# The down projection of a hybrid transformer block, transposed and with Strassen's scheme for every other pair of row tiles

## The chip, the cores and the metric

The kernel runs on one core of a Trainium2 chip. The core has five engines with a queue of instructions each: TensorE (PE) multiplies matrices, VectorE (DVE) and ScalarE (ACT) work on elements, GpSimd (POOL) does a little of the same, and SyncE (SP) issues most of the DMAs. The metric is the device time in microseconds. Three runs of the kernel before took 2153.89, 2154.22 and 2154.32 us; the median is 2154.22.

## The reference, cut to what matters

One block: RMSNorm, an input projection, a short convolution and a windowed attention side by side, an output projection with residual, then the MLP and a last norm. The change touches the MLP only:

```python
h = rms_norm(h_res, norm2_g[l])
h_res = h_res + jnp.square(jax.nn.relu(h @ w_up[l])) @ w_down[l]
out = rms_norm(h_res, final_norm_g)
```

There are 512 tokens, 2048 features and 8192 hidden features, all in fp32.

## The kernel before

Every fp32 operand is split in two parts that PE multiplies fast: a rounded one (hi, a CAST on ACT, line 182) and what is left (lo, a subtraction on DVE, line 183). A product takes three matmuls, hi x hi, hi x lo and lo x hi, which add up in one PSUM bank.

The up projection runs over 32 groups of 256 hidden features (`n`). A group takes four steps (`s`) over 512 input features each. A step loads one slab of weights, 512 KB (`load`, line 159, from SP), into one of three slots (`raw`), and uses one level of Strassen's scheme: DVE forms four sums of weight blocks (lines 747 to 749), ACT and DVE split the three blocks that are used as they are (`q`) and the four sums (`wsp`), and PE makes seven products of 128 x 128 weights with 256 tokens for each of two pairs of row tiles (lines 766 to 770). The operand on the token side stands ready in SBUF, eight pairs in eight places (`sobuf`, `xa`, `xc`). At the end of a group `up_out` combines four PSUM banks into the four quarters of the output (lines 778 to 786), applies relu and square on ACT (787, 788) and writes them to DRAM from ACT's queue (789, `a_d`, 512 KB). The banks alternate between two sets of four, `mm` and `aux`.

The down projection runs in eight chunks of eight row tiles, by four column blocks of 512 features. Its weights are the moving operand: a product takes 128 tokens of the activations as weights of the array and 512 features as columns (`mm3`, lines 633 to 635). The activations come back from `a_d` and are split once for each chunk. At the end of a chunk and column block DVE adds the banks to the residual `acc`, scaled by token (line 852). The last chunk also makes the sums of squares for the last norm and stores the output.

The order of the instructions on each engine is fixed before the run by the framework's list scheduler, which also hands out the slots of the rings: a slot goes to the tiles in the order in which they ask for it. On the chip each engine takes its instructions in that order. In the tables of instructions below `u12_3` is PSUM bank 3 of group 12, `raw_up13_0` the weights of group 13, step 0, as loaded, `q3` and `wsp` the split weights, `xq` and `ctmp` the buffers in which a group's output is combined.

Of the kernel before, what the change touches and what calls it, by code (L numbers as in the profile page):

```python
# [8 lines left out]
F32 = mybir.dt.float32  # L9
# [4 lines left out]
P = 128  # L14
D = 2048
# [84 lines left out]
def hybrid_block_kernel(  # L100
# [53 lines left out]
    wring = {}  # L154


    def load(src, name):
        raw = wring["raw"].next(name)
        wring["last"] = nc.sync.dma_start(raw, src)
        return raw  # L160

# [205 lines left out]


    xap = tc.alloc_tile_pool(name="xap", bufs=1, side="left")
    xa_hi = xap.tile([P, 8, SEQ], F32R, name="xa_hi")  # L370
    xa_lo = xap.tile([P, 8, SEQ], F32R, name="xa_lo")
    xe = tc.alloc_tile_pool(name="xe", bufs=1, side="left")
    xc2 = []

    def xc_tiles(pool, n):
        for i in range(n):
            f = len(xc2)
            hi = pool.tile([P, 2, SEQ], F32R, name=f"xc_hi{f}")
# [346 lines left out]
    a_d = [dram.tile([P, 4 * HT], F32, name=f"a_d{n}") for n in range(NG)]  # L725


    PROD = {
# [9 lines left out]

    by4 = lambda v, n=4: v.rearrange("p (m s c) -> p m s c", m=2, s=n)

    def up_slab(n, s):
        raw = load(w_up[n, s], f"up{n}_{s}")
# [7 lines left out]
        t_hi, t_lo = (by4(v) for v in part_tiles(f"up{n}_{s}"))  # L750
        split(t_hi, t_lo, t)
        return (q_hi, q_lo), (t_hi, t_lo)

    def up_step(bs, n, s):
        both = up_slab(n, s)
        for k in range(2):
            m = 2 * s + k
            for q, (sm, w, x, b, c) in PROD.items():
                o = bs[b][:, c * HT : (c + 1) * HT]
                h, l = (v[:, k, w, :] for v in both[sm])  # L760
                xh, xl = (operand[m][x][:, i, :] for i in range(2))
                first = m == 0 and q in (1, 2, 3, 5)
                if q == 5:

                    x2 = operand[m][x].rearrange("p h c -> p (h c)")
                    nc.tensor.matmul(bs[b], lhsT=h, rhs=x2, start=first, stop=False, skip_group_check=True)  # L766
                else:
                    nc.tensor.matmul(o, lhsT=h, rhs=xh, start=first, stop=False, skip_group_check=True)  # L768
                    nc.tensor.matmul(o, lhsT=h, rhs=xl, start=False, stop=False, skip_group_check=True)  # L769
                nc.tensor.matmul(o, lhsT=l, rhs=xh, start=False, stop=m == NPR - 1, skip_group_check=True)  # L770

    def up_out(bs, n):


        e, u = E.next()
        e, u = (v.rearrange("p (s c) -> p s c", c=HT) for v in (e, u))
        two = lambda v: v.rearrange("p (a b) -> p a b", a=2)
        nc.scalar.copy(u[:, 0, :], bs[2][:, :HT])
        nc.vector.tensor_tensor(u[:, 1, :], bs[0][:, :HT], u[:, 0, :], op=ALU.add)
        nc.vector.tensor_tensor(e[:, 0, :], bs[2][:, HT:], u[:, 1, :], op=ALU.add)  # L780
        nc.scalar.copy(e[:, 2, :], bs[3][:, HT:])
        nc.vector.tensor_tensor(e[:, 2, :], bs[3][:, :HT], e[:, 2, :], op=ALU.add)
        nc.vector.tensor_tensor(e[:, 1, :], e[:, 2, :], u[:, 1, :], op=ALU.subtract)
        nc.vector.tensor_tensor(e[:, 2, :], e[:, 2, :], e[:, 0, :], op=ALU.subtract)
        nc.vector.tensor_tensor(e[:, 3, :], bs[0][:, HT:], u[:, 0, :], op=ALU.add)
        nc.vector.tensor_tensor(e[:, 0:2, :], two(bs[1]), e[:, 0:2, :], op=ALU.add)
        nc.scalar.activation(e, e, AF.Relu)
        nc.scalar.activation(e, e, AF.Square)
        nc.scalar.dma_start(a_d[n], e.rearrange("p s c -> p (s c)"))
# [17 lines left out]
    xcp.release()  # L807
    xe.release()
    xap.release()
    wp2 = ctx.enter_context(tc.tile_pool(name="wp2", bufs=1, side="left"))  # L810
    wring["raw"] = Ring(*raw_slots(3, wp), *raw_slots(2, wp2))
    wring["split"] = Ring(*split_slots(3, wp), *split_slots(3, wp2))
    A = Ring(*[lambda name, i=i: part(sobuf, 2048, i) for i in range(7)])
    pf = ctx.enter_context(tc.tile_pool(name="pf", bufs=1, side="left"))
    gF = pf.tile([P, D], F32, name="gF")
    sq = pf.tile([P, NT, 5], F32, name="sq")
    junk = [pf.tile([P, 512], F32, name=f"junk{i}") for i in range(2)]

    QUART = {(1, 1): 0, (0, 0): 1, (1, 0): 2, (0, 1): 3}
    tags = ["mm", "aux"]  # L820
    turn = 0
    for ch in range(NCHUNK):
        a_hi, a_lo = [], []
        last = ch == NCHUNK - 1
        k0 = ch * FCH
        if last:
            with tc.issue_after(wring["last"].ins):
                nc.sync.dma_start(gF, final_g.partition_broadcast(P))
        for i in range(3 if last else 4):
            bs = [bank(tags[turn], f"d{ch}_{i}_{t}") for t in range(NT)]  # L830
            turn ^= 1
            for s_ in range(0, FCH, 2):
                if i == 0:

                    n = 4 * ch + s_ // 2
                    both = A.next()
                    split(both[:, 0:1024], both[:, 1024:2048], load(a_d[n], f"a{n}"))
                    for b in range(2):
                        for lst, c in ((a_hi, 0), (a_lo, 1024)):
                            lst.append([both[:, c + QUART[t // 2, b] * HT + t % 2 * P :][:, :P] for t in range(NT)])  # L840
                wh, wl = slab(w_down[i, (k0 + s_) // 2], 512, f"dn{ch}_{i}_{s_}")
                if ch == 0 and s_ == 2:

                    with tc.issue_after(wring["last"].ins):
                        nc.sync.dma_start(accs[i], acc_d[i])
                for k in range(2):
                    kt = s_ + k
                    for t in range(NT):
                        mm3(bs[t], a_hi[kt][t], a_lo[kt][t], wh[:, k, :], wl[:, k, :], kt == 0, kt == FCH - 1)
            for t in range(NT):  # L850
                a = acc(i, t)
                nc.vector.scalar_tensor_tensor(a, bs[t], rs2[:, t : t + 1], a, op0=ALU.mult, op1=ALU.add)  # L852

                if last:
# [7 lines left out]
    for t in range(NT):  # L862
# [89 lines left out]
```

## Time and profile before

| | |
|---|---|
| median of the runs | 2154.22 us |
| the profiled execution | 2152.87 us |
| its span, first to last instruction | 2151.1 us |
| PE busy | 2138.4 us (99%), 13404 matmuls |
| DVE busy | 1294.5 us (60%) |
| ACT busy | 810.3 us (38%) |
| POOL busy | 141.0 us (7%) |
| DMA | 261.29 MB, 121 GB/s |

Busy times are sums over the whole span, and the span has several stages. Matmuls are pipelined: a record of one lasts longer than the step from one start to the next, so the rate is counted from the number of matmuls in a stretch. The up projection lies about between 801 and 1445 us, the down projection between 1445 and 2142 us.

### The profile page before, as it was taken

How to read it: one execution, taken by the hardware profiler on the slowest of the kernel's cores; microseconds unless marked ns; L12 is line 12 of the kernel's file. 1: busy time of each engine (PE TensorE's matmuls, PEld its weight loads, DVE VectorE, ACT ScalarE, POOL GpSimd, SP SyncE). 2: the span in 40 equal slices, each digit the busy share in tenths (PEclk: the TensorE clock that was granted, in tenths of full speed). 3: DMA queues.
4: the chain of work that ended last, by engine and by line, in shares of the span. 5: the costliest groups of instructions: out<-in, count | busy, mean ns of one | idle time of the engine just before them, and what ended most of it. 6: DMA issues, size and time to landing. Idle time of an engine off the chain costs nothing.

```text
span 2151.1 us, 32786 instructions
## 1 busy us (share of the span) xinstructions
PE 2138.4 (99%) x13404; PEld 1940.3 (90%) x13404; DVE 1294.5 (60%) x2047; ACT 810.3 (38%) x1142; POOL 141.0 (7%) x256
## 2 busy tenths in 40 slices
PE   9999999999999999999999999999999999999998
PEld 8999999999988889999999999998888888888887
DVE  7776766443435569888888888874444343434434
ACT  6455544222212335545545545552222222222223
POOL 1432321001110000000000000000000000000001
PEclk9999999999999999999999999999999999999999
DMA  5322222222253334434334334355343333433422
GB/s 193 91 91 82 75 87 75 92 94 92 96 167 108 118 120 135 138 128 137 130 126 138 133 123 137 138 194 218 117 134 105 125 127 108 137 118 118 148 88 79
DMA packets 89996, 261.29 MB, mean 121 GB/s; under 512 B 25637, under 2 KB 25717, under 8 KB 88693
## 3 DMA queue, kind: packets, MB, share of 16 engines
q1 hardware_dynamic: 84660, 238.22, 33.6%
q10 hardware_dynamic: 4608, 16.78, 1.9%
q0 software_dynamic: 576, 4.19, 0.5%
q8 instruction: 105, 1.72, 0.3%
q14 instruction: 47, 0.38, 0.1%
HBM read 233.99 MB, written 25.17 MB: 120 GB/s over the span
## 4 chain that ended last, share of the span: by engine, by line
PE 98%; POOL 1%; SPq 0%; DMA 0%; ACT 0%; issue 0%; POOLq 0%; ACTq 0%; DVE 0%
PE d L633 10%; PE d L634 10%; PE d L635 10%; PE u L770 10%; PE u L768 9%; PE u L769 9%; PE u L766 3%; PE mm_u L211 1%; PE mm_c L211 1%; PE mm_u L208 1%; PE mm_c L208 1%; PE mm_u L209 1%; PE mm_c L209 1%; PE mm_b L211 1%; PE mm_b L208 1%; PE mm_b L209 1%
## 5 line engine op out<-in xcount | busy, mean ns | idle before, releaser
L633 PE MATMUL d<-wsp_dn,sobuf 128*128 128x512 f32 x992 | 385.9, 389 | 0.0
L634 PE MATMUL d<-wsp_dn,sobuf 128*128 128x512 f32 x992 | 385.9, 389 | 0.0
L635 PE MATMUL d<-wsp_dn,sobuf 128*128 128x512 f32 x992 | 385.9, 389 | 0.0
L183 DVE TENSOR_TENSOR wsp_dn<-raw_dn,wsp_dn 128x1024 fp32r<-128x1024 f32 x124 | 151.7, 1224 | 267.2 <-ACT wsp_dn L182 267.1
L182 ACT CAST wsp_dn<-raw_dn 128x1024 fp32r<-128x1024 f32 x124 | 130.6, 1054 | 379.4 <-PE d L635 375.0
L635 PEld LDWEIGHTS d<-wsp_dn,sobuf 128*128 128x128 f32 x992 | 186.2, 188 | 38.7
L633 PEld LDWEIGHTS d<-wsp_dn,sobuf 128*128 128x128 f32 x992 | 186.2, 188 | 38.7
L634 PEld LDWEIGHTS d<-wsp_dn,sobuf 128*128 128x128 f32 x992 | 186.2, 188 | 38.6
L182 ACT CAST q<-raw_up 128x768 fp32r<-128x768 f32 x128 | 106.8, 835 | 234.9 <-PE u L769 165.3
L183 DVE TENSOR_TENSOR wsp_up<-tsum,wsp_up 128x1024 fp32r<-128x1024 f32 x128 | 156.7, 1224 | 44.2 <-ACT wsp_up L182 43.9
L182 ACT CAST wsp_up<-tsum 128x1024 fp32r<-128x1024 f32 x128 | 134.3, 1049 | 69.7 <-PE u L770 60.9
L183 DVE TENSOR_TENSOR q<-raw_up,q 128x768 fp32r<-128x768 f32 x128 | 122.4, 956 | 41.6 <-ACT q L182 41.6
L770 PE MATMUL u<-sobuf,wsp_up 128*128 128x256 f32 x512 | 144.9, 283 | 0.0
L769 PE MATMUL u<-sobuf,q 128*128 128x256 f32 x384 | 108.9, 284 | 0.0
L768 PE MATMUL u<-sobuf,wsp_up 128*128 128x256 f32 x384 | 108.6, 283 | 0.0
L768 PE MATMUL u<-sobuf,q 128*128 128x256 f32 x384 | 108.4, 283 | 0.0
L769 PE MATMUL u<-sobuf,wsp_up 128*128 128x256 f32 x384 | 108.4, 282 | 0.0
L770 PE MATMUL u<-sobuf,q 128*128 128x256 f32 x384 | 108.3, 282 | 0.0
L852 DVE SCALAR_TENSOR_TENSOR acc<-d,few,acc 128x512 f32<-128x512 f32 x124 | 86.1, 748 | 24.0 <-PE d L635 24.0
L183 DVE TENSOR_TENSOR sobuf<-raw_a,sobuf 128x1024 fp32r<-128x1024 f32 x32 | 39.2, 1225 | 101.4 <-ACT sobuf L182 101.4
L770 PEld LDWEIGHTS u<-sobuf,wsp_up 128*128 128x128 f32 x512 | 97.1, 190 | 0.0
L747 DVE TENSOR_TENSOR tsum<-raw_up 128x512 f32<-128x512 f32 x128 | 88.1, 688 | 2.9 <-DMA raw_up<-in_w_up_dram 1.0
(319 smaller groups left out, 5469.9 us busy)
## 6 DMA issues: line engine op xcount, KB each, us to landing
raw_up<-in_w_up_dram SPq DMA_DIRECT2D x128, 512.0 KB
raw_dn<-in_w_down_dram SPq DMA_DIRECT2D x124, 512.0 KB
a_d<-xq ACTq DMA_DIRECT2D x32, 512.0 KB
raw_a<-a_d SPq DMA_DIRECT2D x32, 512.0 KB
raw_q<-in_w_in_dram SPq DMA_DIRECT2D x16, 512.0 KB
raw_u<-in_w_in_dram SPq DMA_DIRECT2D x16, 512.0 KB
raw_c<-in_w_in_dram SPq DMA_DIRECT2D x16, 512.0 KB
raw_b<-in_w_in_dram SPq DMA_DIRECT2D x16, 512.0 KB
```

The costliest lines, as they stand in the source:

```text
L182: first = nc.scalar.copy(hi, src)
L183: second = nc.vector.tensor_tensor(lo, src, hi.bitcast(F32), op=ALU.subtract)
L208: nc.tensor.matmul(b, lhsT=wh, rhs=cols(h_hi, kt), start=kt == 0, stop=False)
L209: nc.tensor.matmul(b, lhsT=wh, rhs=cols(h_lo, kt), start=False, stop=False)
L633: nc.tensor.matmul(o, lhsT=ah, rhs=wh, start=start, stop=False)
L634: nc.tensor.matmul(o, lhsT=ah, rhs=wl, start=False, stop=False)
L635: nc.tensor.matmul(o, lhsT=al, rhs=wh, start=False, stop=stop)
L747: nc.vector.tensor_tensor(t[:, :, 0:2, :], b12, w[:, :, 1:3, :], op=ALU.add)
L768: nc.tensor.matmul(o, lhsT=h, rhs=xh, start=first, stop=False, skip_group_check=True)
L769: nc.tensor.matmul(o, lhsT=h, rhs=xl, start=False, stop=False, skip_group_check=True)
L770: nc.tensor.matmul(o, lhsT=l, rhs=xh, start=False, stop=m == NPR - 1, skip_group_check=True)
L852: nc.vector.scalar_tensor_tensor(a, bs[t], rs2[:, t : t + 1], a, op0=ALU.mult, op1=ALU.add)
```

## The change

The first 24 of the 32 pairs of hidden row tiles (three quarters) leave the old chunks; chunks 6 and 7 stay as they were. For the 24 pairs the product is transposed: the weights are the array's weights and 256 or 512 tokens the columns, so that the result has features on the partitions.

- Eight column groups (`G`) of 256 features are visited in turn, 24 visits. Visit `v` takes group `v % 8` and the eight pairs `v` to `v + 7` (modulo 24), so that three visits of a group cover all pairs. From one visit to the next the set slides by one pair: `down_operand` loads and splits one new pair into the place of the old one.
- Even pairs go by Strassen's scheme: seven products of 256 columns with three matmuls each, with weight sums made by the function that made them for the up projection. Odd pairs go plainly, with products of 512 columns. A visit has two steps of each kind, with two pairs in a step: 84 matmuls of 256 columns and 48 of 512.
- `down_out` combines the four banks; the results add up in eight tiles `accT`. In chunk 6, 64 transposes (16 x 4) bring them back to tokens on partitions, and a second update for each bank adds them to `acc`.
- In the up projection, `up_out` keeps its operations, with the quarters in another order. After an even group below 24, POOL forms four combinations of the quarters, in a tile taken from the ring of the weight slots (`xs`), and writes them to DRAM from POOL's queue.
- In the last up group, the operands of the first eight pairs are loaded between its steps, also through the three weight slots.
- Buffers of the rest move: chunks 6 and 7 use parts of `xq` and `xa` as slots, and the last gain and scratch tiles lie where `xc` was.

```diff
+    NPD = 24
+    by_scheme = lambda n: n % 2 == 0
@@ up_out, after relu and square
+        nc.scalar.dma_start(a_d[n][:, :1024], e.rearrange("p s c -> p (s c)"))
+        if n < NPD and by_scheme(n):
+            raw = wring["raw"].next(f"xs{n}")
+            xs = by_q(raw)
+            nc.gpsimd.tensor_tensor(xs[:, 0, :], e[:, 0, :], e[:, 1, :], op=ALU.subtract)
+            nc.gpsimd.tensor_tensor(xs[:, 1, :], xs[:, 0, :], e[:, 2, :], op=ALU.subtract)
+            nc.gpsimd.tensor_tensor(xs[:, 2, :], e[:, 2, :], e[:, 0, :], op=ALU.subtract)
+            nc.gpsimd.tensor_tensor(xs[:, 3, :], e[:, 3, :], xs[:, 1, :], op=ALU.add)
+            nc.gpsimd.dma_start(a_d[n][:, 1024:], raw)
...
+    def down_operand(n):
+        if by_scheme(n):
+            v = places[n % NW // 2][0][2]
+            r = load(a_d[n][:, 256:1024], f"da{n}", 768)
+            split(v[:, 0:3, 0, :], v[:, 0:3, 1, :], by_q(r))
+            r = load(a_d[n][:, 1024:], f"ds{n}")
+            split(v[:, 3:7, 0, :], v[:, 3:7, 1, :], by_q(r))
+        else:
+            r = wring["raw"].next(f"da{n}")
...
+            both = whole[n % NW // 2]
+            split(both[:, 0:1024], both[:, 1024:2048], r)
...
+    def down_step(bs, pairs, G, begun, last, name):
+        raw = wring["raw"].next(name)
+        for k, n in enumerate(pairs):
+            wring["last"] = nc.sync.dma_start(
...
+        if by_scheme(pairs[0]):
+            both = step_slab(raw, name)
+            for k, n in enumerate(pairs):
+                ops = places[n % NW // 2][0][2]
+                for q, (sm, w, x, _, _) in PROD.items():
...
+                    mm(b, o, h, xh)
+                    mm(b, o, h, xl)
+                    mm(b, o, l, xh, last and k == 1)
+        else:
...
+                for e in range(2):
+                    xh, xl = (v[:, i * 1024 + e * 512 :][:, :512] for i in range(2))
+                    for j in range(2):
+                        b = 1 if j else 3
+                        mm(b, bs[b], hi[:, k, e, j, :], xh)
+                        mm(b, bs[b], hi[:, k, e, j, :], xl)
+                        mm(b, bs[b], lo[:, k, e, j, :], xh, last and k == 1 and e == 1)
...
         for s_ in range(4):
             up_step(bs, n, s_)
+            for m in {0: (0, 2), 1: (4, 6), 2: (1, 3, 5, 7)}.get(s_, ()) if n == NG - 1 else ():
+                down_operand(m)
         up_out(bs, n)
+    for v in range(NPD):
+        G = v % 8
+        bs = banks(v)
+        begun = set()
+        at = lambda *d: [(v + i) % NPD for i in d]
+        for s_, d in enumerate(((0, 2), (1, 3), (4, 6), (5, 7))):
+            down_step(bs, at(*d), G, begun, s_ > 1, f"dt{v}_{s_}")
+            if s_ == 0 and v + 1 < NPD:
+                down_operand((v + 8) % NPD)
...
+        if v < 8:
...
+            down_out(bs, accT[G], u)
+        else:
+            down_out(bs, e, u)
+            nc.vector.tensor_tensor(accT[G], accT[G], e, op=ALU.add)
...
+                if ch == first_ch:
+                    pt = bank(tags[turn], f"pt{i}_{t}")
+                    for k in range(4):
+                        v = accT[2 * i + k // 2][:, QUART_T[t // 2, k % 2], t % 2 * P : (t % 2 + 1) * P]
+                        nc.tensor.transpose(pt[:, k * P : (k + 1) * P], in_=v, identity=ident)
+                    nc.vector.scalar_tensor_tensor(a, pt, rs2[:, t : t + 1], a, op0=ALU.mult, op1=ALU.add)
```

The order on ACT where group 12 ends and group 13 begins. Before:

```order
L182 CAST q3_2_7852<-raw_up13_0_10699 128x768
L789 DMA a_d11_7866<-xq_6616 128x1024
L182 CAST wsp_up13_0_10706<-tsum_7850 128x1024
L182 CAST q3_3_7853<-raw_up13_1_10749 128x768
L182 CAST wsp_up13_1_10756<-tsum_7850 128x1024
L182 CAST q3_1_7851<-raw_up13_2_10799 128x768
L781 COPY xq_6616<-u12_3_10482 128x256
L778 COPY ctmp_7854<-u12_2_10481 128x256
L182 CAST wsp_up13_2_10806<-tsum_7850 128x1024
```

The same place on ACT in the changed kernel (its relu and square are lines 792 and 793):

```order
L786 COPY xq_6616<-u12_3_10518 128x256
L783 COPY ctmp_7854<-u12_2_10517 128x256
L792 ACTIVATE xq_6616<-xq_6616 128x1024
L793 ACTIVATE xq_6616<-xq_6616 128x1024
L794 DMA a_d12_7867<-xq_6616 128x1024
L182 CAST q3_2_7852<-raw_up13_0_10741 128x768
L182 CAST wsp_up13_0_10748<-tsum_7850 128x1024
L182 CAST q3_3_7853<-raw_up13_1_10791 128x768
```

Before, casts for three slabs of group 13 stand ahead of the first copy of group 12's output. Now the copies, relu, square and the DMA of group 12 stand ahead of the first cast of group 13.

The same place on DVE in the changed kernel, from the last split of group 12's weights:

```order
L183 TENSOR_TENSOR wsp_up12_3_10676<-tsum_7850,wsp_up12_3_10676 128x1024
L787 TENSOR_TENSOR xq_6616<-u12_3_10518,xq_6616 128x256
L784 TENSOR_TENSOR ctmp_7854<-u12_0_10515,ctmp_7854 128x256
L790 TENSOR_TENSOR xq_6616<-u12_0_10515,ctmp_7854 128x256
L785 TENSOR_TENSOR xq_6616<-u12_2_10517,ctmp_7854 128x256
L788 TENSOR_TENSOR xq_6616<-xq_6616,ctmp_7854 128x256
L789 TENSOR_TENSOR xq_6616<-xq_6616 128x256
L791 TENSOR_TENSOR xq_6616<-u12_1_10516,xq_6616 128x512
L751 TENSOR_TENSOR tsum_7850<-raw_up13_0_10741 128x2x256
L752 TENSOR_TENSOR tsum_7850<-tsum_7850,raw_up13_0_10741 128x2x128
L183 TENSOR_TENSOR q3_2_7852<-raw_up13_0_10741,q3_2_7852 128x768
```

The whole output of group 12 (lines 784 to 791) now stands ahead of all work on group 13's weights. After the odd groups, and after groups from 24 on, the two are interleaved as before.

The order on SP in the last up group of the changed kernel (`da` and `ds` are the two halves of a pair's operand):

```order
L159 DMA raw_up31_0_14659<-in_w_up_dram 128x1024
L159 DMA raw_da0_14709<-a_d0_7855 128x768
L159 DMA raw_ds0_14713<-a_d0_7855 128x1024
L159 DMA raw_da2_14717<-a_d2_7857 128x768
L159 DMA raw_ds2_14721<-a_d2_7857 128x1024
L159 DMA raw_up31_1_14725<-in_w_up_dram 128x1024
L159 DMA raw_da4_14775<-a_d4_7859 128x768
L159 DMA raw_ds4_14779<-a_d4_7859 128x1024
L159 DMA raw_da6_14783<-a_d6_7861 128x768
L159 DMA raw_ds6_14787<-a_d6_7861 128x1024
L159 DMA raw_up31_2_14791<-in_w_up_dram 128x1024
```

Before, the slabs of the last group follow each other. Now four operand loads stand between one slab and the next, and all use the three slots.

## Rows read from the trace of the kernel before

**Rows 1.** The page's chain that ended last, by engine.

```profile
PE 98%; POOL 1%; SPq 0%; DMA 0%; ACT 0%; issue 0%; POOLq 0%; ACTq 0%; DVE 0%
```

**Rows 2.** Windows of both projections: length, busy us (instructions) by engine, clock, DMA.

```profile
820.00:1440.00 620.00, 620.00 (x4942) 609.03 (x4941) 522.06 (x839) 316.92 (x376) 0.00 (x0) 1.00 0.39 134
1460.00:2100.00 640.00, 640.00 (x2825) 529.96 (x2824) 261.07 (x271) 156.15 (x161) 0.63 (x2) 1.00 0.37 125
```

**Rows 3.** Timeline of PE at its transposes: start, length, instruction.

```profile
672.81 1.04 PE L666 MATMUL p2t<-ident,acc 128*128 128x128 f32 x8
673.68 0.39 PE L656 MATMUL ps<-diag,ones 128*128 128x128 f32 x2
```

**Rows 4.** The page's groups: busy us, mean ns, idle before. The update.

```profile
L852 DVE SCALAR_TENSOR_TENSOR acc<-d,few,acc 128x512 f32<-128x512 f32 x124 | 86.1, 748 | 24.0 <-PE d L635 24.0
```

**Rows 5.** Groups of DVE, 1000 to 1480 us.

```profile
L183 DVE TENSOR_TENSOR wsp_up<-tsum,wsp_up 128x1024 fp32r<-128x1024 f32 x87 | 106.5, 1225 | 34.4 <-ACT wsp_up L182 34.2
L183 DVE TENSOR_TENSOR q<-raw_up,q 128x768 fp32r<-128x768 f32 x86 | 82.2, 956 | 29.0 <-ACT q L182 29.0
L747 DVE TENSOR_TENSOR tsum<-raw_up 128x512 f32<-128x512 f32 x85 | 58.5, 689 | 1.5
L748 DVE TENSOR_TENSOR tsum<-tsum,raw_up 128x256 f32<-128x256 f32 x85 | 36.0, 423 | 2.2
...
L786 DVE TENSOR_TENSOR xq<-u,xq 128x512 f32<-128x512 f32 x23 | 15.7, 684 | 0.0
```

**Rows 6.** Timeline of PE: the next group's first product.

```profile
1003.47 0.28 PE L768 MATMUL u<-sobuf,q 128*128 128x256 f32 x1
```

**Rows 7.** Timeline of ACT, 1000 to 1030 us.

```profile
1002.12 0.83 ACT L182 CAST q<-raw_up 128x768 fp32r<-128x768 f32 x1 [2.43 <-PE u L769]
...
1003.67 0.37 ACT L778 COPY ctmp<-u 128x256 f32<-128x256 f32 x1 [0.34 <-PE u L770]
...
1012.16 0.83 ACT L182 CAST q<-raw_up 128x768 fp32r<-128x768 f32 x1 [0.33 <-PE u L769]
1012.17 0.33 ACTq L789 DMA_DIRECT2D a_d<-xq  x1
```

**Rows 8.** Timeline of DVE, 1000 to 1030 us.

```profile
1002.99 0.96 DVE L183 TENSOR_TENSOR q<-raw_up,q 128x768 fp32r<-128x768 f32 x1 [0.39 <-ACT q L182]
...
1004.86 0.41 DVE L780 TENSOR_TENSOR xq<-u,ctmp 128x256 f32<-128x256 f32 x1
1005.19 0.42 DVE L783 TENSOR_TENSOR xq<-xq,ctmp 128x256 f32<-128x256 f32 x1
```

**Rows 9.** Groups of ACT, 1000 to 1480 us.

```profile
L182 ACT CAST wsp_up<-tsum 128x1024 fp32r<-128x1024 f32 x86 | 90.2, 1049 | 45.6 <-PE u L770 45.6
...
L788 ACT ACTIVATE xq<-xq 128x1024 f32<-128x1024 f32 x23 | 24.4, 1061 | 0.7
L787 ACT ACTIVATE xq<-xq 128x1024 f32<-128x1024 f32 x23 | 24.2, 1052 | 0.0
```

**Rows 10.** Groups of POOL, operations of 256 columns.

```profile
L445 POOL TENSOR_TENSOR s<-bt,msk 128x256 f32<-128x256 f32 x32 | 28.1, 880 | 78.2 <-PE yb L511 77.9 <-POOL pm L478 0.3
...
L549 POOL TENSOR_TENSOR ub<-ub,rs_bc 128x256 f32<-128x256 f32 x8 | 11.5, 1434 | 0.0
```

**Rows 11.** The tile acc_d: writes of 1024 KB, from issue to landing.

```profile
L678 POOL DMA_DIRECT2D acc_d<-acc x4: 533/566/781, 665.2 to 804.1; - x4
...
DMA to landing us min/median/max: 4.4/4.6/4.9
```

**Rows 12.** Windows behind the last product; the clock stands after five engines.

```profile
2142.00:2143.00 1.00, 0.04 (x1) 0.00 (x0) 0.48 (x1) 0.34 (x2) 0.00 (x0) 1.00 1.06 393
...
2145.00:2146.00 1.00, 0.00 (x0) 0.00 (x0) 0.30 (x1) 0.76 (x2) 0.00 (x0) 0.94 0.00 0
2146.00:2147.00 1.00, 0.00 (x0) 0.00 (x0) 0.00 (x0) 0.00 (x0) 0.00 (x0) 0.50 0.78 201
```

**Rows 13.** Timeline of PE at the start of the span.

```profile
1.42 2.39 PE L239 MATMUL pg<-ident 128*128 128x128 f32 x10 [1.42 <-POOL ident masks.py:199]
```

More of the change, by code (lines that the diff above doesn't have):

```diff
@@ L154, in hybrid_block_kernel, with load @@
     wring = {}
-    def load(src, name):
-        raw = wring["raw"].next(name)
+    def load(src, name, n=SLAB):
+        raw = wring["raw"].next(name)[:, :n]
         wring["last"] = nc.sync.dma_start(raw, src)
@@ L724, in hybrid_block_kernel @@
     E = Ring(*[lambda name, i=i: (part(flat(xq), 1024, i), ctmp[:, i, :]) for i in range(2)])
-    a_d = [dram.tile([P, 4 * HT], F32, name=f"a_d{n}") for n in range(NG)]
+    NPD = 24
+    by_scheme = lambda n: n % 2 == 0
+    a_d = [dram.tile([P, (8 if n < NPD and by_scheme(n) else 4) * HT], F32, name=f"a_d{n}") for n in range(NG)]
     PROD = {
@@ L770, in up_step @@
                 nc.tensor.matmul(o, lhsT=l, rhs=xh, start=False, stop=m == NPR - 1, skip_group_check=True)
+    by_q = lambda v: v.rearrange("p (s c) -> p s c", c=HT)
+    two = lambda v: v.rearrange("p (a b) -> p a b", a=2)
     def up_out(bs, n):
-        e, u = E.next()
-        e, u = (v.rearrange("p (s c) -> p s c", c=HT) for v in (e, u))
-        two = lambda v: v.rearrange("p (a b) -> p a b", a=2)
+        e, u = (by_q(v) for v in E.next())
         nc.scalar.copy(u[:, 0, :], bs[2][:, :HT])
@@ new lines, in hybrid_block_kernel @@
+    NW = 8
+    OPD = (1, 2, 6, 0, 3, 4, 5)
+    whole = [flat(t)[:, i * 2048 : (i + 1) * 2048] for t in (xa_hi, xa_lo) for i in range(2)]
+    def down_operand(n):
[7 more added lines that the diff above has]
+            r = wring["raw"].next(f"da{n}")
+            q = r.rearrange("p (b h c) -> p b h c", b=2, c=HT)
+            nc.sync.dma_start(q[:, :, 0, :], two(a_d[n][:, 512:1024]))
+            wring["last"] = nc.sync.dma_start(q[:, :, 1, :], two(a_d[n][:, 0:512]))
+            both = whole[n % NW // 2]
+            split(both[:, 0:1024], both[:, 1024:2048], r)
@@ new lines, in parts_flat, with down_out @@
+    def parts_flat(raw, name):
+        hi, lo = part_tiles(name)
+        split(hi, lo, raw)
+        return hi, lo
+    def down_out(bs, e, u):
+        nc.scalar.copy(e[:, 0, :], bs[2][:, :HT])
+        nc.vector.tensor_tensor(u, bs[0][:, :HT], e[:, 0, :], op=ALU.add)
+        nc.vector.tensor_tensor(e[:, 1, :], bs[2][:, HT:], u, op=ALU.add)
+        nc.vector.tensor_tensor(e[:, 2, :], bs[0][:, HT:], u, op=ALU.subtract)
+        nc.vector.tensor_tensor(e[:, 3, :], bs[0][:, HT:], e[:, 1, :], op=ALU.subtract)
+        nc.vector.tensor_tensor(e[:, 0:2, :], two(bs[1]), e[:, 0:2, :], op=ALU.add)
+        nc.vector.tensor_tensor(e[:, 2:4, :], two(bs[3]), e[:, 2:4, :], op=ALU.add)
@@ new lines, in hybrid_block_kernel @@
+    accT = []
+    ED = Ring(*[lambda name, i=i: (by_q(part(flat(xq), 1024, i)), part(sqc, HT, i)) for i in range(2)])
+    for v in range(NPD):
[7 more added lines that the diff above has]
+                down_operand((v + 8) % NPD)
+        e, u = ED.next()
+        if v < 8:
+            t = acc_pools[G].tile([P, 2, SEQ], F32, tag=f"xc_{('hi', 'lo')[G % 2]}{G // 2}", name=f"accT{G}")
+            accT.append(by_q(flat(t)))
+            down_out(bs, accT[G], u)
+        else:
+            down_out(bs, e, u)
+            nc.vector.tensor_tensor(accT[G], accT[G], e, op=ALU.add)
@@ L813, in hybrid_block_kernel @@
+    accs = acc_tiles()
+    raws = [part(flat(xq), 1024, i) for i in range(2)]
+    wring["raw"] = Ring(*raw_slots(3, wp), *[lambda name, v=v: v for v in raws])
+    wring["split"] = Ring(*split_slots(3, wp), *[lambda name, v=v: v for v in whole])
     A = Ring(*[lambda name, i=i: part(sobuf, 2048, i) for i in range(7)])
-    pf = ctx.enter_context(tc.tile_pool(name="pf", bufs=1, side="left"))
-    gF = pf.tile([P, D], F32, name="gF")
+    pf = ctx.enter_context(tc.tile_pool(name="pf", bufs=1, side="right"))
```

76 lines of the change are left out of this document (46 added, 30 removed).

## The prediction

> **What bounds the kernel now.** I read the chain of waits first: 98% of the span stands on PE [rows 1]. Then the stretches: in the middle of the up projection and of the down projection PE is busy the whole time, at the full clock, while DVE has 522 of 620 us in the first and 261 of 640 us in the second [rows 2]. So a matmul saved is time saved, and a wait that reaches PE is time lost. The second thing to see is how narrow the up projection is: DVE is 84% busy there, and PE never waits only because DVE and ACT prepare weights about two steps ahead.
>
> The steps of PE come from the same two rows. Down: 640 us / 2825 products of 512 columns = 0.2265 us. Up: of 21 column blocks of 256 a group of 20 products holds, so 4942 products are 5189 blocks, and 620 / 5189 = 0.1195 us for a block. Half of a wide product would be 0.113, so narrow products cost 5% extra.
>
> **The saving.** The 24 pairs took 24 x 96 wide products. Now there are 24 visits with 84 narrow and 48 wide ones each: 84 x 0.1195 + 48 x 0.2265 = 20.9 us against 96 x 0.2265 = 21.7, so -0.84 us a visit, **-20.0 us** in all. Added are 64 transposes: eight of that shape took 672.81 to 673.68, 0.109 us each [rows 3], **+7.0 us**. Around them the banks that the transposes use are the next set's, and each is released by a DVE update of 0.75 us [rows 4]; the order on PE has filled most of this with other products. I put **+6 us** for these waits and for the start of chunk 6, whose loads wait for the last visit's buffers (0 if all is filled; 16 updates x 0.75 = 12 if none is).
>
> In the visits themselves I expect no wait. DVE has per visit two scheme slabs of 3.7 us (0.96 + 0.69 + 2 x 0.42 + 1.22 [rows 5]), two plain subtractions of 1.22, one operand (2.2 or 1.2), the output (4 x 0.42 + 2 x 0.68) and the addition into accT (1.2): 15.8 of 20.9 us, and the output of a visit stands in DVE's order behind one or two prepared slabs of the next.
>
> **What the change moves: twelve full stops.** The diff doesn't show this, the order does. Before, ACT casts the weights of group 13 three slabs deep before it copies the outputs of group 12, and DVE does the same. After, in every even group from 0 to 22 (those that write the four combinations, which now take a slot of the ring of weights), all of group n's output stands ahead of the first cast of group n+1 on ACT, and ahead of its first subtraction on DVE. PE has nothing of its own between the two groups. So PE stands still from the last product of group n until this has run, one after the other, none of it beside PE's work:
>
> - ACT's copy starts 0.20 us after the place where PE's next product would be (1003.67 against 1003.47 [rows 6, 7]) and takes 0.37.
> - DVE: five operations of 256 columns, then one of 512. Independent ones follow at 0.33 us, two of the steps wait for the one ahead (0.42 + 0.04; the 0.04 is what DVE starts behind ACT's cast, 1002.12 + 0.83 to 1002.99 [rows 7, 8]): 3 x 0.33 + 2 x 0.46 + 0.68 = 2.6.
> - ACT: relu and square, 1.05 + 1.06 [rows 9]; then the DMA's issue, which waits for the square and stands ahead of the cast, 0.33 [rows 7]; then the cast, 0.83.
> - Six handovers of 0.04.
>
> Sum 0.20 + 0.37 + 2.6 + 2.1 + 0.33 + 0.83 + 0.24 = 6.7 us. Then PE restarts with nothing prepared: behind the cast come 0.96 + 0.42 on DVE, the cast of the sums 1.05 on ACT, 1.22 on DVE, with handovers 3.8 us, and PE has products for 17 blocks, 2.0 us, in that time: 1.7 more. The combinations are late too: four operations on POOL at 0.88 to 1.43 us [rows 10], a write and then the load of slab 3, each between half and all of the 4.6 us that a transfer twice as large takes [rows 11]. That lands some 16 us after the stop's beginning; PE wants slab 2, whose cast is queued behind it, at about 19. This the stop itself covers.
>
> The clock is the last part. Behind the kernel's last product, at 2142.0, the granted level is still 0.94 in the slice from 2145 and 0.50 in the next [rows 12]: it fell while PE idled, for less long than a stop lasts. At the start ten transposes took 2.39 us, 0.24 each, against the 0.109 of later [rows 3, 13], so PE is slow for its first microseconds of work. In a stop's aftermath most of that time is spent waiting on casts anyway; I put +0.9. One stop: 6.7 + 1.7 + 0.9 = 9.3 us, twelve: **+112 us**. Bounds for one: 5.0 (all DVE and ACT steps at their closest spacing, no restart cost) and 13 (the whole first slab of 42 blocks at the half level, +5.0, less what overlaps with the waits). I take the middle because the terms below it are all single rows.
>
> The Trainium skill ("TensorE: Matmul & The Clock Gate", section "HAM oscillation — how this bites in real kernels") tells of a kernel that waits between short groups of matmuls and finds its clock at half rate in every one of them. By that rule each stop would end in a slow restart, nearer to the upper bound. The same page ("Architectural detail") has ACT and DVE as strictly first in, first out, which is what the stop rests on; in the trace of before the ACT rows run in the order of the program, and nothing there overtakes.
>
> **The hand-over to the visits: +22 us.** Around the last group's four slabs stand the operands of eight pairs, twelve halves through the same three slots. Each step's slab is loaded into a slot that an operand holds, and that operand may only be written once PE has finished the step that reads its place. So from step to step: last product, cast 1.05, subtraction 1.22, load (2.3 to 4.6), cast 0.83, and the slow restart of 1.7, about 8 us; a part of the first is hidden, as place 0 is free half a step early. Three steps, 22 us; 10 if the loads are at the low end and overlap, 35 at the high end.
>
> **Sum.** Against the profiled execution (2152.9 us: span 2151.1 and 1.8 around it; the median of the runs is 1.3 higher): -20.0 + 7.0 + 6 + 22 + 112 = +127, so 2280, and 2281 on the median's scale.
>
> **Rivals.**
> - *The stops do not reach PE.* If the first casts of group n+1 ran before relu and square, PE would restart at once, and the hand-over would be filled likewise: 2154 - 20 + 7 + 6 = 2147, faster. It needs less than (20 - 13) / 12 = 0.6 us per stop and no hand-over. For it: PE 98% of the chain, nothing waits now [rows 1]. Against: the order is fixed, and one ACT queue runs it. 6%.
> - *Shallow stops.* 5.0 to 6.7 us each, the restart hidden because the sums are formed while ACT still works, hand-over 10: 2154 - 7 + 70 + 10 = 2227. 16%.
> - *Deep stops.* The clock halves in each and stays so for the first slab, and slab 3's load comes late: 12.5 us each, hand-over 30: 2154 - 7 + 150 + 30 = 2327. The slices at the end show the fall but not the time to come back [rows 12]. 18%. By the Trainium skill's rule above ("TensorE: Matmul & The Clock Gate") this would be the likely one.
> - *My forecast*, stops of 8 to 11 us: 60%, with 2255 to 2305.
>
> The range that leaves out 2 in 10: 2228 to 2325. About 0.2% (4 us) is what runs of this kernel can tell from no change. Only the first rival is on the other side: faster 0.05, same 0.02, slower 0.93.
>
> **What would show it.** PE's idle time in the up projection, in twelve pieces of 6 to 7 us before the first product of the odd groups, each ended by ACT's cast of q (line 182); the granted clock below 1 in these slices; some 20 us of idle PE in group 31; PE whole in the visits, 20.9 us each. If PE shows no idle pieces at the odd groups, my main term is wrong; if visits take over 22 us, the saving is.

## The result, and the profile after

The changed kernel takes **2313.3 us** (median of 4 runs, 2311.9 to 2319.2) against 2154.1 us for the kernel before on the same chip: 1.0745 times as long, 95% interval 1.0732 to 1.0759. The forecast was 2281 us with a range of 2228 to 2325. The direction, the place and the mechanism were as forecast; the size of one stop and of the hand-over was too small.

The chain of waits, by engine, answers to [rows 1]:

```profile
PE 69%; DMA 12%; DVE 10%; ACT 4%; issue 2%; SPq 2%; POOL 1%; ACTq 0%; DVEq 0%; POOLq 0%
```

PE holds 69% of this chain instead of 98%. The windows of the up projection (ten pairs of groups) and of the visits answer to [rows 2]: start and end, length, busy us of PE, PEld, DVE, ACT and POOL (instructions), granted clock, DMA share, GB/s.

```profile
900.00:1413.00 513.00, 440.52 (x3208) 427.83 (x3207) 338.15 (x543) 200.95 (x241) 41.82 (x50) 0.90 0.33 114
1640.00:2060.00 420.00, 420.00 (x2643) 381.84 (x2642) 283.90 (x403) 148.86 (x170) 0.00 (x0) 1.00 0.43 135
```

In the up projection PE now stands still for 72 of 513 us and the clock's mean is 0.90; in the visits it is busy all the time at the full clock (1.00). Two rows of the page's groups (busy us, mean ns of one, idle time just before them and who ended it) say what PE waited for in each:

```profile
L772 PE MATMUL u<-sobuf,q 128*128 128x256 f32 x384 | 120.2, 314 | 77.1 <-ACT q L182 77.1
...
L844 PE MATMUL u<-sobuf,wsp_dt 128*128 128x256 f32 x1152 | 154.3, 283 | 1.6 <-ACT wsp_dt L182 1.6
```

Line 772 with `sobuf` and `q` begins the first two steps of an up group: eleven pieces of 6.5 us stand before the odd groups 3 to 23 and one of 5.6 us inside group 31. The twelfth stop, 6.6 us, is ahead of the last step of group 1, whose steps are interleaved with group 0's. One stop, the seventh, on ACT (start, length, instruction; in brackets the idle time before and its releaser); it answers to [rows 7]:

```profile
1133.43 0.37 ACT L783 COPY ctmp<-u 128x256 f32<-128x256 f32 x1 [0.28 <-PE u L774]
1136.47 1.06 ACT L792 ACTIVATE xq<-xq 128x1024 f32<-128x1024 f32 x1 [2.67 <-DVE xq L791]
1137.56 1.06 ACT L793 ACTIVATE xq<-xq 128x1024 f32<-128x1024 f32 x1
1138.64 0.33 ACTq L794 DMA_DIRECT2D a_d<-xq  x1
1139.01 0.83 ACT L182 CAST q<-raw_up 128x768 fp32r<-128x768 f32 x1 [0.40 <-ACT xq L793]
1141.83 1.05 ACT L182 CAST wsp_up<-tsum 128x1024 fp32r<-128x1024 f32 x1 [1.99 <-DVE tsum L753]
```

Here the output of the even group (copy, relu, square, the DMA's issue) runs first, and only then the cast that PE waits for. The weights that it casts had been loaded before: DVE forms its first sums from the same slab at 1136.35 (below), 2.7 us ahead of the cast. So it is the order on ACT that holds PE here, not a missing load. Why the list scheduler chooses this order when `xs` takes a slot is not shown. On DVE beside it, answering to [rows 5, 8], and on POOL, answering to [rows 10]:

```profile
1136.35 0.68 DVE L751 TENSOR_TENSOR tsum<-raw_up 128x512 f32<-128x512 f32 x1
1137.07 0.42 DVE L752 TENSOR_TENSOR tsum<-tsum,raw_up 128x256 f32<-128x256 f32 x1
1139.88 1.05 DVE L183 TENSOR_TENSOR q<-raw_up,q 128x768 fp32r<-128x768 f32 x1 [2.38 <-ACT q L182]
1140.85 0.95 DVE L753 TENSOR_TENSOR tsum<-tsum,raw_up 128x256 f32<-128x256 f32 x1
1141.72 1.21 DVE L751 TENSOR_TENSOR tsum<-raw_up 128x512 f32<-128x512 f32 x1
```

```profile
1138.70 0.72 POOL L800 TENSOR_TENSOR raw_xs<-xq 128x256 f32<-128x256 f32 x1 [46.64 <-ACT xq L793]
1139.39 0.71 POOL L802 TENSOR_TENSOR raw_xs<-xq 128x256 f32<-128x256 f32 x1
1140.08 1.44 POOL L801 TENSOR_TENSOR raw_xs<-raw_xs,xq 128x256 f32<-128x256 f32 x1
1141.60 0.79 POOL L803 TENSOR_TENSOR raw_xs<-xq,raw_xs 128x256 f32<-128x256 f32 x1
```

Compare DVE's sum of 512 columns (line 751) and its sums of 256 (lines 752 and 753): 0.68 and 0.42 us while POOL is idle, 1.21 and 0.95 beside POOL's combinations. The windows around the same stop answer to [rows 12]; the clock stands behind POOL's column:

```profile
1131.00:1133.00 2.00, 2.00 (x19) 1.95 (x18) 0.00 (x0) 0.23 (x1) 0.00 (x0) 1.00 0.00 0
1133.00:1138.00 5.00, 0.39 (x4) 0.19 (x2) 3.98 (x9) 2.02 (x4) 0.00 (x0) 1.00 0.00 0
1138.00:1140.00 2.00, 0.10 (x1) 0.10 (x1) 0.12 (x1) 1.45 (x2) 1.30 (x2) 0.52 0.28 115
...
1142.00:1144.00 2.00, 1.26 (x5) 0.97 (x5) 2.00 (x2) 1.61 (x2) 0.97 (x2) 0.50 0.46 119
1144.00:1146.00 2.00, 2.00 (x11) 2.00 (x10) 2.00 (x5) 0.76 (x2) 0.00 (x0) 0.50 0.97 399
1146.00:1148.00 2.00, 2.00 (x11) 2.00 (x10) 2.00 (x4) 1.02 (x2) 0.00 (x0) 0.50 0.14 21
1148.00:1150.00 2.00, 2.00 (x16) 1.96 (x16) 0.95 (x2) 0.00 (x0) 0.00 (x0) 0.92 0.95 358
```

The clock falls to 0.50 (the 1.2 GHz level) in the stop and stays there for some 8 us behind the restart: 11 products in 2 us instead of 19.

**Where the time went** (spans 2311.3 and 2151.1, a difference of 160.2 us). A pair of groups, between ACT's copies of line 783 from group 3 to group 23, takes 51.19 us against 40.16: 11.03 a stop, 132.4 for twelve. Group 31 takes 48.48 us between its copies against 20.10: 28.4. These are its windows, before and after, and PE's waits in the second:

```profile
1425.35:1445.45 20.10, 20.10 (x161) 19.72 (x160) 12.28 (x17) 11.47 (x14) 0.00 (x0) 1.00 0.67 231
```

```profile
1561.18:1609.66 48.48, 32.29 (x197) 30.09 (x196) 30.22 (x40) 22.43 (x25) 0.00 (x0) 0.79 0.55 177
```

```profile
PE u L772 <- ACT q L182: 13.7, 3, 5.5
PE u L772 <- ACT wsp_up L182: 2.4, 2, 1.9
```

PE stands still for 16.2 us of it; the rest is the lower clock and the first products of visit 0, which run ahead of the second copy. From there to the last visit's copy are 502.8 us, against 522.4 for three quarters of the old stage: -19.6. From the last visit's copy to the last product are 189.7 us against 174.1 for the last quarter: 15.6, of which the transposes are 7.0 and one stop of 7.4 us at the start of chunk 6 the next. Before the MLP 3.4 us were lost in the attention stage (a 2.5 us wait of PE there). Sum 160.2.

### The profile page after: what moved, and what is told of

Same layout as the page of the kernel before. It is cut to its first block, busy times and chain, and to the rows that moved or that the text cites. A ratio compares the mean times of both kernels' runs of the same rounds, so it can differ in the third digit from the quotient of the medians.

```text
span 2311.3 us, 35375 instructions
## 1 busy us (share of the span) xinstructions
PE 2185.1 (95%) x14332; PEld 2021.1 (87%) x14332; DVE 1447.9 (63%) x2342; ACT 871.0 (38%) x1237; POOL 191.9 (8%) x316
## 4 chain that ended last, share of the span: by engine, by line
PE 69%; DMA 12%; DVE 10%; ACT 4%; issue 2%; SPq 2%; POOL 1%; ACTq 0%; DVEq 0%; POOLq 0%
DMA raw_dt<-in_w_down_dram 10%; PE u L774 9%; PE u L772 8%; PE u L773 8%; PE u L770 3%; PE d L633 2%; PE d L634 2%; PE d L635 2%; DVE wsp_dt L183 2%; DVE q L183 2%; SPq L838 2%; PE mm_u L211 1%; PE mm_c L211 1%; PE mm_u L208 1%; PE mm_c L208 1%
## 5 line engine op out<-in xcount | busy, mean ns | idle before, releaser
L772 PE MATMUL u<-sobuf,q 128*128 128x256 f32 x384 | 120.2, 314 | 77.1 <-ACT q L182 77.1
L844 PE MATMUL u<-sobuf,wsp_dt 128*128 128x256 f32 x1152 | 154.3, 283 | 1.6 <-ACT wsp_dt L182 1.6
L772 PEld LDWEIGHTS u<-sobuf,q 128*128 128x128 f32 x384 | 82.9, 216 | 79.6 <-ACT q L182 79.6
L844 PEld LDWEIGHTS u<-sobuf,wsp_dt 128*128 128x128 f32 x1152 | 145.3, 192 | 1.9 <-ACT wsp_dt L182 1.9
L774 PE MATMUL u<-sobuf,wsp_up 128*128 128x256 f32 x512 | 138.8, 298 | 0.0
L844 PE MATMUL u<-xa_lo,wsp_dt 128*128 128x512 f32 x576 | 136.8, 390 | 0.0
L844 PE MATMUL u<-xa_hi,wsp_dt 128*128 128x512 f32 x576 | 136.6, 390 | 0.0
L844 PEld LDWEIGHTS u<-xa_hi,wsp_dt 128*128 128x128 f32 x576 | 107.0, 188 | 21.5
L844 PEld LDWEIGHTS u<-xa_lo,wsp_dt 128*128 128x128 f32 x576 | 106.9, 188 | 21.6 <-ACT wsp_dt L182 0.2
L772 PE MATMUL u<-sobuf,wsp_up 128*128 128x256 f32 x384 | 116.1, 304 | 8.8 <-ACT wsp_up L182 8.8
L844 PE MATMUL u<-sobuf,q 128*128 128x256 f32 x864 | 120.0, 284 | 0.0
L773 PE MATMUL u<-sobuf,q 128*128 128x256 f32 x384 | 118.4, 309 | 0.0
L844 PEld LDWEIGHTS u<-sobuf,q 128*128 128x128 f32 x864 | 113.6, 193 | 3.0 <-ACT q L182 0.2
L773 PE MATMUL u<-sobuf,wsp_up 128*128 128x256 f32 x384 | 114.1, 299 | 0.0
L774 PE MATMUL u<-sobuf,q 128*128 128x256 f32 x384 | 112.2, 307 | 0.0
L787 DVE TENSOR_TENSOR xq<-u,xq 128x256 f32<-128x256 f32 x32 | 13.4, 420 | 131.9 <-ACT xq L786 131.9
```

Of the source, the lines that this page charges most:

```text
L844: nc.tensor.matmul(o, lhsT=w, rhs=x, start=b not in begun, stop=stop, skip_group_check=True)
```

## The experiments

Per stop, the loss is read in every run in the same way: the period of a pair of groups (copies of groups 3 to 23) less 40.16. A change in the total says less of a stop: from group 31's copy to the end the profiled executions of the change and of five runs with the same visits take between 701.6 and 710.5 us.

| run | us (median) | ratio to before, 95% interval | pair of groups | lost per stop |
|---|---|---|---|---|
| the change | 2313.3 | 1.0732 to 1.0759 | 51.19 | 11.03 |
| own places | 2181.2 | 1.0116 to 1.0146 | 40.13 | 0 |
| before, with the slot alone | 2284.4 | 1.0593 to 1.0625 | 50.97 | 10.81 |
| filled stops | 2305.6 | 1.0691 to 1.0723 | 50.22 | 10.06 |
| copies | 2288.4 | 1.0606 to 1.0638 | 49.39 | 9.23 |
| copies and filled stops | 2288.3 | 1.0614 to 1.0645 | 48.88 | 8.72 |
| long copies | 2300.2 | 1.0664 to 1.0700 | 49.81 | 9.65 |

**Own places.** The combinations leave the ring of weights:

```diff
-            raw = wring["raw"].next(f"xs{n}")
-            xs = by_q(raw)
+            xs = [v[:, i * HT : (i + 1) * HT] for v in (sqc, s_bc) for i in range(2)]
...
-            nc.gpsimd.dma_start(a_d[n][:, 1024:], raw)
+            nc.gpsimd.dma_start(a_d[n][:, 1024:1536], sqc)
+            nc.gpsimd.dma_start(a_d[n][:, 1536:], s_bc)
```

> The combinations get places of their own (the idle sum of squares tile and the idle scale row) and no slot of the weights' ring; GpSimd's arithmetic and its output stay. Theory: the slot alone orders group n's whole output ahead of group n+1's first weights, so the twelve stops of 6.5 us and the half clock behind them go, 12 x 11.05 us = 132.6 us: 2313 - 133 = about 2181 us (2172 to 2190), intervals between outputs 20.1 us in every group, clock 1.00 through the up stage. Rival: the combinations themselves (GpSimd's work slowing VectorE to half, or their late writes) make the stops, which then stay: 2290 to 2315 us.

Measured: 2181.2 us (2179.1 to 2186.6), 132.1 less than the change. The window of the up projection up to the hand-over, as in [rows 2]:

```profile
820.00:1425.00 605.00, 605.00 (x4822) 594.30 (x4821) 525.52 (x815) 304.73 (x363) 62.80 (x72) 1.00 0.43 141
```

PE never waits there, at the full clock. ACT's order is again the one of before, though POOL still makes the combinations; group 12's copies stand between casts of weights:

```profile
1062.15 0.83 ACT L182 CAST q<-raw_up 128x768 fp32r<-128x768 f32 x1 [2.43 <-PE u L773]
1063.03 0.37 ACT L786 COPY xq<-u 128x256 f32<-128x256 f32 x1
1063.70 0.37 ACT L783 COPY ctmp<-u 128x256 f32<-128x256 f32 x1 [0.30 <-PE u L774]
1063.97 1.05 ACT L182 CAST wsp_up<-tsum 128x1024 fp32r<-128x1024 f32 x1
```

The slot makes the stops; the combinations by themselves cost nothing when PE has weights ahead.

**The slot alone, in the kernel before:**

```diff
         nc.scalar.dma_start(a_d[n], e.rearrange("p s c -> p (s c)"))
+        if n < 24 and n % 2 == 0:
+            raw = wring["raw"].next(f"xs{n}")
...
+            nc.gpsimd.dma_start(x_d[n // 2], raw)
```

> The kernel before, with nothing added but the combinations of the even groups 0 to 22 in a slot of the weights' ring, on GpSimd, and their output to a place that nobody reads; the down projection is the one of before. Theory: the twelve stops come with it: 2154 + 133 = 2287 us (2275 to 2297). Rival: the stops need something else of the change (its other order of sums in the output, its memory layout): 2154 to 2165 us.

Measured: 2284.4 us, +130.1. The waits of PE (total, times, longest):

```profile
PE u L769 <- ACT q L182: 78.4, 12, 6.8
PE u L769 <- ACT wsp_up L182: 9.1, 12, 0.9
```

The twelve stops come without the new down projection. With the run before this settles the cause from both sides.

**Filled stops.** Is the half clock what makes a stop dearer than its 7.2 us of idle time (6.5 before the restart and 0.74 behind it)?

```diff
     def up_step(bs, n, s):
+        if s == 0 and 1 < n < NPD and not by_scheme(n):
+            for i in range(54):
+                h = held[0][0][:, 1, 3, :]
+                nc.tensor.matmul(bs[0][:, :HT], lhsT=h, rhs=operand[7][0][:, 0, :], start=True, stop=True)
```

> The order and the stops' causes stay, but eleven of the twelve stops (before groups 3, 5 to 23) are filled with 54 products of 256 columns whose result is overwritten. Theory: TensorE's clock then stays at full level, and what a stop costs beyond its 7.3 us of idle time, 3.75 us, is saved: 11 x 3.75 = 41 us, 2272 us (2262 to 2285). Rival: behind a stop TensorE is held by late weights anyway and the half clock costs nothing by itself: 2305 to 2320 us, with idle pieces behind the filling.

Measured: 2305.6 us, 7.7 less; the theory expected 41 less, and the rival was right. The window of ten pairs and PE's waits in it:

```profile
900.00:1413.00 513.00, 493.40 (x3815) 476.58 (x3814) 346.66 (x557) 204.16 (x246) 42.00 (x50) 0.99 0.35 116
```

```profile
PE u L780 <- ACT wsp_up L182: 13.3, 10, 1.3
PE u L782 <- DVE wsp_up L183: 4.2, 6, 1.3
```

The clock is up (0.99 against 0.90), and PE uses the speed to arrive sooner at weights that aren't there: the wait of 0.74 us behind each stop becomes 1.33, and behind six of the ten another appears two steps on. Half speed and late weights cover each other; a stop loses 0.97 us less, no more. For eleven stops that is 10.7 us; that the total is only 7.7 lower comes from outside them (behind the up projection this profiled execution is 6.8 us longer than that of the change).

**Copies.** Does POOL's work beside DVE make a stop dearer?

```diff
-            nc.gpsimd.tensor_tensor(xs[:, 0, :], e[:, 0, :], e[:, 1, :], op=ALU.subtract)
+            nc.gpsimd.tensor_copy(xs[:, 0, :], e[:, 0, :])
...
```

> The changed kernel with GpSimd's four combinations replaced by four copies of as many columns (the combinations' values are left out); the slot and nearly all of the order stay. Theory: VectorE's operations in the stop (0.95 and 1.21 us there, 0.42 and 0.69 elsewhere) are slowed by GpSimd's reading two operands, so with copies they take 0.42 and 0.69 again and each stop is 1.0 us shorter, 5.5 us: 2313 - 12 = 2301 us. Rival: any GpSimd work, or the place itself, slows them: 6.5 us and 2309 to 2316 us.

Measured: 2288.4 us, 25 less. The stop itself stayed at 6.5 us, so the expectation was wrong on the place: what ends the stop is ACT's cast, not DVE. What shrank is the time behind it: DVE's two sums take 0.42 and 0.68 in every group, and the wait of 0.74 us falls to 0.2. In the seventh stop the clock is back some 3.9 us after the restart instead of 8.4; over the ten stops of the table it is 3.4 to 6.2 us, 5.0 on average. A stop loses 1.80 us less, 21.6 for twelve; the rest of the 25 lies outside the stops (the 3.4 us of the attention stage are not in this profiled execution). This run doesn't show whether copies slow DVE, because POOL has done its last copy before DVE's first sum:

```profile
1125.76 0.41 POOL L803 COPY raw_xs<-xq 128x256 f32<-128x256 f32 x1
```

```profile
1126.89 0.41 DVE L753 TENSOR_TENSOR tsum<-tsum,raw_up 128x256 f32<-128x256 f32 x1
1127.23 0.68 DVE L751 TENSOR_TENSOR tsum<-raw_up 128x512 f32<-128x512 f32 x1
```

**Copies and filled stops**, both edits together:

> The run with copies instead of combinations, and in it the eleven stops filled with 54 products as in the run with filled stops (the combinations' values are left out). Theory: what ate the full clock's gain in the filled run was the weights' lateness that GpSimd's combinations make; without it a filled stop costs its 6.7 us of filling and about 0.5, against 9.2 with copies alone: 2288 - 11 x 2 = about 2266 us (2260 to 2274). Rival: the weights are late because the order leaves nothing prepared, whatever GpSimd does: 2280 to 2290 us.

Measured: 2288.3 us, nothing less in all, and 0.51 us less per stop than with copies alone; the rival was right again. PE's waits in ten pairs:

```profile
PE u L780 <- ACT wsp_up L182: 7.9, 10, 0.8
PE u L782 <- DVE wsp_up L183: 0.9, 2, 0.7
```

At full clock (1.00) and without POOL's combinations a stop still costs 8.72: 6.64 of filling, and 2.1 behind it, where PE meets weights that the order has left unprepared. The filling ahead of group 13:

```profile
1119.20 6.64 PE L765 MATMUL u<-xc_lo,wsp_up 128*128 128x256 f32 x54
```

**Long copies.** Two things went with the combinations: POOL's weight on DVE, and 2.3 us in which the slot was held (from 1.4 to 3.7 us). Ten copies instead of four were to hold it about as long as the combinations:

```diff
-            nc.gpsimd.tensor_copy(xs[:, 0, :], e[:, 0, :])
+            for _ in range(3):
+                nc.gpsimd.tensor_copy(xs[:, 0, :], e[:, 0, :])
...
```

> The run with copies, but the first three copies made three times each, ten in all, so that GpSimd holds the slot about as long as with the combinations (3.5 us against 3.7; the combinations' values are left out). Theory 1: the 25 us that the copies saved came of the slot given back 2 us earlier: it is lost again, 2306 to 2316 us. Theory 2: they came of VectorE, no longer slowed to half: still 2285 to 2293 us.

Measured: 2300.2 us, between the two. Per stop 9.65, so 0.42 of the 1.80 comes back. The ten copies took 6.0 us and not the 3.5 expected (from 1127.52 to 1133.56 in the stop below), longer than the combinations, because from the fifth on they ran beside DVE. They aren't free of DVE, as I had assumed; these are DVE's sums and some of POOL's copies behind one restart:

```profile
1129.68 0.61 DVE L753 TENSOR_TENSOR tsum<-tsum,raw_up 128x256 f32<-128x256 f32 x1
1130.21 0.88 DVE L751 TENSOR_TENSOR tsum<-raw_up 128x512 f32<-128x512 f32 x1
```

```profile
1128.54 0.41 POOL L806 COPY raw_xs<-xq 128x256 f32<-128x256 f32 x1
1128.88 1.13 POOL L801 COPY raw_xs<-xq 128x256 f32<-128x256 f32 x1
1129.96 0.59 POOL L803 COPY raw_xs<-xq 128x256 f32<-128x256 f32 x1
```

Each side is slower beside the other. The slot was held 4.6 us longer than with four copies, and a stop cost 0.42 us more: so the held slot is worth at most 0.4 us a stop. At least 1.4 of the 1.8 came with the combinations beside DVE: DVE's sums were slower with them (0.95 and 1.21 against 0.61 and 0.88 here), and the half clock lasted longer (8.3 to 8.9 us behind the restart, against 3.6 to 7.0 here). With the clock kept up, the copies are worth 10.06 - 8.72 = 1.3 us a stop, so most of it is not the clock. About half of this run's 12 us over the copies lies behind the up projection, not in the stops.

**The hand-over**, on top of own places. The first eight pairs' operands come through five idle pieces of 512 columns, by POOL's queue:

```diff
+    OQ = Ring(*[lambda name, v=v: v for v in [t[:, 1536:2048].bitcast(F32) for t in q3] + [sqc, s_bc]])
...
+                r = OQ.next(f"da{n}_{i}")[:, : (j - i) * HT]
+                nc.gpsimd.dma_start(r, a_d[n][:, (i + 1) * HT : (j + 1) * HT])
...
-            for m in {0: (0, 2), 1: (4, 6), 2: (1, 3, 5, 7)}.get(s_, ()) if n == NG - 1 else ():
-                down_operand(m)
+            for m in {1: (0, 2)}.get(s_, ()) if n == NG - 1 else ():
+                first_operand(m)
...
+            for n in d if v == 0 and s_ else ():
+                first_operand(n)
```

> As the run with own places, and the operands of the first eight pairs come by GpSimd's queue through five idle pieces of 512 columns instead of the three slots of the weights' ring, those for visit 0's second to fourth step asked for as late as each step. Theory: in group 31 the slots are what is short: of the 28.4 us lost there 15 go (10 to 25), about 2166 us. Rival: VectorE's 13.6 us of splits for these operands are what is short, in group 31 and visit 0 alike: 2176 to 2186 us, no better than own places alone by more than 5 us.

Measured: 2162.0 us (2161.2 to 2164.3), 19.2 less than own places; 1.0038 times before, interval 1.0023 to 1.0052. Group 31 takes 21.66 us instead of 49.20, but six of the eight pairs are now split in visit 0. So the fair stretch is from group 30's copy to the copy of visit 0, in which all eight are split in both runs (own places first):

```profile
1425.14:1488.39 63.25, 45.66 (x271) 41.48 (x270) 41.38 (x56) 30.28 (x35) 0.00 (x0) 0.87 0.57 180
```

```profile
1425.04:1468.55 43.51, 40.29 (x281) 37.77 (x280) 34.96 (x58) 28.89 (x44) 14.64 (x27) 0.96 0.74 235
```

It is 19.7 us shorter. So DVE's splits were not what held it. The edit changed the slots, the queue and the time of asking together; these were not told apart, so that it was the slots is argued from the order on SP.

**Chunk 6**, on top of the hand-over:

```diff
+    r3, x2 = raw_slots(3, wp), [lambda name, v=v: v for v in raws]
-    wring["raw"] = Ring(*raw_slots(3, wp), *[lambda name, v=v: v for v in raws])
+    wring["raw"] = Ring(*r3, x2[0])
...
+            if ch == first_ch and i == 1:
+                wring["raw"] = Ring(x2[1], *r3, x2[0])
...
-                if ch == first_ch and s_ == 2:
+                if ch == first_ch and s_ == 6:
```

> As the run with the hand-over, and at the start of chunk 6 the third activation slab (group 26) takes one of the three ordinary slots instead of the one that the last visit's output holds, and the residual's reloads are asked for two slabs later. Theory: the 8.2 us stop there came of that slot (and its queue), so it goes with the half clock behind it: 2162 - 8.2 - 1.5 = about 2152 us (2149 to 2157), level with the kernel before or just under. Rival: the transfers at the start of chunk 6 (about 380 GB/s) are themselves the bound and the stop only moves: 2158 to 2164 us.

Measured: 2155.2 us (11 runs, 2150.4 to 2158.8), 1.0005 times before, interval 0.9996 to 1.0014: no difference from the kernel before, and 6.8 us less than the hand-over, within the theory's range. The stop of 8.2 us is now one of 1.5, ended by DVE's update of a bank that the transposes use.

**The operand later**, on top of chunk 6:

```diff
-            if s_ == 0 and v + 1 < NPD:
+            if s_ == 2 and v + 1 < NPD:
                 down_operand((v + 8) % NPD)
```

> As the run on chunk 6, and each visit asks for the operand of the pair that slides in behind its third step instead of its first (it is needed in the next visit's last step). Theory: the waits of 0.4 to 0.9 us at the starts of ten later visits, 4.6 us in all, come of VectorE's splits for it standing ahead of the next weights, and go: 4 us under the run on chunk 6, about 2148 us, and under the kernel before. Rival: VectorE's total of 29 us in 42 us with the outputs' 4 us in one piece is the cause, whatever the place: within 1 us of the run on chunk 6, or worse by up to 4 us.

Measured: 2146.0 us (2143.1 to 2147.0), 0.9963 times before, interval 0.9950 to 0.9975: **this version beats the kernel before**, by 0.4%. It is 9.2 us under the run on chunk 6, more than the 4 expected, and by the profiled executions not for the reason given. In that of the run on chunk 6 the waits of the later visits came to about 1 us only. What went is the hand-over's: three waits of 3.9 us in visit 0 (at 1457.7, 1458.9 and 1461.8), with a clock of 0.90 from 1447 to 1480, where this run has no wait and 1.00. Its windows, as in [rows 2], and all that PE waits for from 820 to 2110 us:

```profile
820.00:1440.00 620.00, 620.00 (x4942) 609.04 (x4941) 546.52 (x850) 319.92 (x384) 71.92 (x89) 1.00 0.45 146
1460.00:1940.00 480.00, 480.00 (x3010) 435.94 (x3010) 327.31 (x468) 174.88 (x201) 0.00 (x0) 1.00 0.44 139
```

```profile
PE d L633 <- DVE acc L1004: 1.8, 1, 1.8
```

The first row has the same 4942 products as before, with the combinations made beside them. The span is 8.3 us shorter than before (2151.1 - 2142.8): the visits' 19.6 less the transposes' 7.0 and some 4 more.

## Why the prediction was right, and where its sizes were off

- **What bounds the kernel: right.** PE did, and each wait that reached it was time. The visits take 20.99 us each (20 of them from 1649.69 to 2069.49; 20.9 forecast), and the stretch is 19.6 us shorter (20.0 forecast). That PE waits nowhere in them from 1625 us on is in part luck of this execution: in the profiled executions of own places and of long copies, with the same visits, it waited 6.2 and 5.7 us there.
- **Twelve full stops: right** in number, cause and releaser, and in place but for one, which lies inside group 1. They were read from the order of the instructions, and the two runs on the slot show that it alone makes them. The bare stop was put at 6.7; it is 6.5.
- **A stop's price: 11.03 us, not 9.3.** The step that failed is "This the stop itself covers", which priced the combinations at nothing. POOL's operations were looked up one by one ([rows 10]), and their landing in memory was reckoned, but not what they do to DVE in the only microseconds in which PE waits for DVE. With copies in their place a stop costs 9.23. The other parts held: 8.72 with the clock kept up, of which 2.1 for the restart (1.7 forecast), and 0.5 to 1.0 for the clock (0.9 forecast).
- **The clock, a point at which the trace and the cost part.** The clock does go to half in every stop and stays there into the next slab, as the rival of deep stops said, and as the Trainium skill ("TensorE: Matmul & The Clock Gate", section "HAM oscillation — how this bites in real kernels") has it for a kernel that waits between groups. But this is worth 0.5 to 1.0 us a stop, as the filled runs show, because weights that come late would hold PE anyway. Later slabs do come late, as that rival also said: behind the seventh stop two casts of ACT waited 1.6 and 3.3 us for loads, but no wait of PE came of it in the change. The measured time lies nearer to that rival's 2327 than to 2281, and mostly not for its reason.
- **The hand-over: 28.4, not 22** (bounds 10 and 35). The loss, where operands and slabs share the same three slots, is what the hand-over run took away. PE's idle time in it is 16.2 us (some 20 forecast); what lies over the sum is the low clock (0.84 on average from 1560 to 1625), for which it had only a restart of 1.7 us a step, and the first products of visit 0, which are counted in the 28.4.
- **Transposes and the start of chunk 6: 15.6, not 13.** The loads did wait for the last visit's buffers, in one stop of 7.4 us, and no wait for the update of the banks shows.
- **Not foreseen:** 3.4 us before the MLP. The wait of 2.5 us is in the profiled execution of the change, with 1.9 and 1.7 in those of the slot alone and of copies with filled stops; in the others it is 0.2 or not there. Its cause stays open.

Together 20.4 + 6.4 + 0.4 + 2.6 + 3.4 = 33.2 us over the forecast terms, of which the twelve stops are the most.

## What to carry to other kernels

A tile that is made late should not share a ring with tiles that are loaded early: slots go out in the order of asking, and here one late owner went with an order that turned a pipeline into a sequence, at 11 us a time. Read it from the order of the instructions before looking at the cost of the operations themselves. And price a stall by what is behind it: keeping the clock up through a stop bought almost nothing as long as the weights behind it were late.

## What the runs showed of the hardware that was not expected

- DVE and POOL slow each other: DVE's sum of 256 columns took 0.95 us instead of 0.42 beside POOL's combinations, and that of 512 columns 1.21 instead of 0.68; beside POOL's copies 0.61 and 0.88, while a copy took 1.13 instead of 0.41. The Trainium skill ("SBUF — State Buffer", section "Who interferes with whom") says that a VectorE operation with two inputs in SBUF contends with a GpSimd operation that reads SBUF. These rows agree, but the size differs: DVE's subtraction of line 183, which has two such inputs too, took 1.05 us beside the combinations instead of 0.95.
- After a stop of 6.5 us the clock stayed at 0.50 for 8.3 to 8.9 us behind the restart in the change, and for 3.4 to 6.2 us with copies, where PE's next wait was 0.2 instead of 0.74 us long. No run tells more about what brings it back.
